# u's second half in split passes, its weights folded by adding transfers, and a table of places for every side step

## The chip, the cores and the metric

The kernel runs on one core of a Trainium2 chip. The metric is the device time in microseconds of one launch. A core has TensorE (PE: matmuls into PSUM; loads of the stationary operand are shown as PEld), VectorE (DVE), ScalarE (ACT), GpSimd (POOL) and the queue engine SyncE (SP). Each engine works off its own instructions in the order in which the program issues them; semaphores order the engines among each other.

## What is computed

One layer of a Fourier token mixer with a gate, for 512 latent tokens and, as a sequence of its own, 128 context tokens; the width is 1024.

```
h    = rms_norm(x, w) * (1 + scale) + shift        # scale, shift, gate = silu(cond) @ w_mod + b_mod
u, z = split(h @ w_in, 2, axis=-1)                 # 1024 columns each
y    = real(fft2(u, over positions and the 256 channels of each of 4 groups)) * silu(z)
x    = x + gate * (y @ w_out)
```

Inputs and outputs are fp32. The attention layer of the reference isn't run (DEPTH is 1).

## The kernel before, in words

**Precision.** PE takes a product of fp32 operands in several passes of its own. The kernel instead splits most operands into a high and a low part of type fp32r (ACT casts the high part, DVE subtracts to get the low one) and runs three passes: high by high, low by high, high by low. `high_piece` and `low_piece` do this for a piece of weights, `plain` and `plain_low` for h, `split_u`, `split_y` and `split_mid` for u, y and the middle channels. Only u's products run on plain fp32 operands (`product_u`, L606).

**Pieces.** The weights are cut into 48 pieces of 128 rows by 512 columns (256 KB): pieces 0 to 7 and 8 to 15 give z's two halves, 16 to 23 and 24 to 31 u's, 32 to 39 and 40 to 47 the output projection. The code's program order is one long list of products by piece `n`, and between them the places `(n, i)`: `run(n, i)` issues there whatever was put in by `at(n, i, step, ...)`. These lists of side steps are written by hand. In z's second half pieces 8 to 11 run one after the other; of 12 to 15 the second token halves of all four column tiles come first (places (12, j) and (13, j)), then the first token halves (places (14, j) and (15, 4j + n - 12)).

**Fold and Fourier transform.** For u the transform over positions is taken ahead of the product with the weights. The tokens (`xn`, five tiles) are scaled by their norms, folded into sums and differences of mirrored positions, four times for 256 columns each (`fold_first`, `fold_context`, `fold_pair`, `fold_cos`, `fold_even`, `fold_sin`), split into fp16 parts (`fold_split`), and `sequence(k)` multiplies 128 columns by the tables (`load_tables`); `evacuate(k)` scales the result into the tile `xs[k]`, 642 columns of bins and shifts. The norms come from `square` (ACT, one for each token tile) and `rms` (POOL). `spread_rms` (L478) writes the 640 norms to DRAM and reads them back as rows, on SP, and `order_rms` (POOL) puts them in order. `shift_products` and `turn_shifts` give the shift term of z; `take_halves` copies z's second half out of PSUM and so frees its banks, of which two serve the first `sequence`.

**u's weights.** u's channels are taken as sums and differences of mirrored channels, so each of its pieces must be folded: `fold_piece` (L202) takes a loaded piece and lets DVE write the sum of its two halves and their difference into one of four slots of the tile `folded`. Before that, `folded` holds rows of weights for `weigh_tile` (DVE, the shift by products and sums, steps 2, 3, 6 and 7). `fold_piece` then issues the load of the piece five further on.

**After u.** `take_u` copies u out of PSUM, `shift_u` adds the mean term, `channels(g)` transforms over the channels, for each of four groups: three passes each for cosine and sine and two for the middle channel (L701), with the high and the low part of `mid`. `channel_out`, `channel_last`, `mix` and `split_y` make the operand of the output projection. `scale_z` and `silu_z` finish z, `weigh_gate` (DVE, with `load_gate`) and `gates` the gate, `results` and `finish_halves` add x and write the result.

## Time and profile before

| | us |
|---|---|
| median of 3 runs | 187.64 (187.57 to 187.74) |
| the profiled execution | 187.82 |
| its span, first to last instruction | 186.0 |
| busy in it: PE, DVE, ACT, POOL | 180.7, 144.9, 87.9, 17.4 |

The profile lists instructions by line and engine with their busy time and mean duration in ns, and what ended the idle time before them. A timeline row reads: start, length, engine, line, operation, output tile <- input tiles, shapes, count, and in brackets the idle time before it with its releaser. In a timeline several like instructions are merged into one row, so that the spacing of rows shows what one really takes from the engine; durations are longer, since the end of one overlaps the start of the next. SPq rows are the issue of a transfer; a transfer's time from issue to landing stands in the list of DMA issues. Stages are marked by the times at which products of new pieces begin.

### The profile page before, as it was taken

What the parts mean: (1) busy time and instruction counts of PE and PEld (TensorE: products, weight loads), DVE (VectorE), ACT (ScalarE), POOL (GpSimd) and SP (SyncE); (2) the same over time, 40 slices, a digit from 0 to 9 for tenths busy, and PEclk for the clock granted to TensorE, in tenths of its full rate; (3) what the DMA queues carried; (4) which work ended last, traced back from release to release, by engine and by line L of the source; (5) the groups of instructions that cost most, each with busy time, mean ns of one, the idle gap of its engine ahead of it and who ended that gap; (6) DMA issues with size and microseconds to landing.
All of it is one profiled execution on the core that took longest, in us unless ns stands there. A gap on an engine that the chain in (4) does not pass through costs nothing.

```text
span 186.0 us, 3224 instructions
## 1 busy us (share of the span) xinstructions
PE 180.7 (97%) x1146; PEld 147.3 (79%) x1146; DVE 144.9 (78%) x319; ACT 87.9 (47%) x199; POOL 17.4 (9%) x56
## 2 busy tenths in 40 slices
PE   7999999999999998999999999999999999999993
PEld 2677777789999988877685786768868889999992
DVE  0544468998999999799998795589869969999422
ACT  3153743359960056977446446778774035210000
POOL 3000000010061005500012031020110000000000
PEclk9999999999999999999999999999999999999999
DMA  5999999999953007843258143120322453703532
GB/s 178 344 406 409 402 402 405 397 389 403 346 156 113 0 10 185 260 188 115 61 221 323 61 113 113 11 104 0 116 60 56 167 176 116 262 16 146 209 119 93
DMA packets 15504, 35.58 MB, mean 191 GB/s; under 512 B 2432, under 2 KB 3200, under 8 KB 15360
## 3 DMA queue, kind: packets, MB, share of 16 engines
q1 hardware_dynamic: 15344, 35.33, 53.8%
q8 instruction: 9, 0.15, 0.4%
q10 hardware_dynamic: 144, 0.04, 0.1%
q14 instruction: 7, 0.06, 0.1%
HBM read 32.75 MB, written 2.62 MB: 190 GB/s over the span
## 4 chain that ended last, share of the span: by engine, by line
PE 73%; DVE 15%; ACT 6%; DMA 3%; issue 2%; SPq 1%; DVEq 0%
PE acc L363 25%; PE acc L610 14%; PE h L400 8%; PE s L400 8%; DVE junk L307 6%; PE acc L373 6%; PE pl L569 3%; DMA zs<-in_w_in 3%; DVE wl L220 3%; PE pm L290 2%; ACT zs L447 1%; PE pc L569 1%; PE acc L618 1%; ACT wh L213 1%; DVE shz L315 1%
## 5 line engine op out<-in xcount | busy, mean ns | idle before, releaser
L610 PE MATMUL acc<-x,folded 128*128 128x324 f32 (+1 forms) x128 | 36.9, 438 | 0.0
L610 PEld LDWEIGHTS acc<-x,folded 128*128 128x128 f32 x128 | 23.5, 190 | 9.6 <-issue 1.0
L220 DVE TENSOR_TENSOR wl<-ws,wh 128x512 fp32r<-128x512 f32 x27 | 18.0, 687 | 2.8 <-ACT wh L213 2.8
L213 ACT CAST wh<-ws 128x512 fp32r<-128x512 f32 x27 | 16.3, 617 | 7.7 <-PE h L400 7.7
L307 DVE SCALAR_TENSOR_TENSOR junk<-wg,cb 128x1024 bf16<-128x1024 f32 x16 | 19.5, 1221 | 0.3
L301 DVE TENSOR_SCALAR a<-pm,b_scale,nw 128x2 f32<-128x2 f32 x8 | 2.2, 278 | 14.6 <-PE pm L300 14.5
L363 PE MATMUL acc<-yh,wh 128*128 128x512 f32 x32 | 13.0, 408 | 0.1
L363 PE MATMUL acc<-yl,wh 128*128 128x512 f32 x32 | 12.6, 394 | 0.0
L363 PE MATMUL acc<-yh,wl 128*128 128x512 f32 x32 | 12.6, 394 | 0.0
L334 ACT ACTIVATE hh<-xt,a 128x128 fp32r<-128x128 f32 (+1 forms) x15 | 7.5, 546 | 9.4 <-DVE a L301 9.4
L400 PE MATMUL h<-yh,wh 128*128 128x256 f32 (+1 forms) x40 | 11.0, 292 | 0.0
L400 PE MATMUL h<-yl,wh 128*128 128x256 f32 (+1 forms) x40 | 11.0, 292 | 0.0
L400 PE MATMUL h<-hl,wh 128*128 128x256 f32 (+1 forms) x40 | 11.0, 292 | 0.0
L400 PE MATMUL h<-hh,wl 128*128 128x256 f32 (+1 forms) x40 | 11.0, 292 | 0.0
L400 PE MATMUL h<-hh,wh 128*128 128x256 f32 (+1 forms) x40 | 11.0, 292 | 0.0
L400 PE MATMUL h<-yh,wl 128*128 128x256 f32 (+1 forms) x40 | 11.0, 291 | 0.0
L363 PE MATMUL acc<-hh,wl 128*128 128x512 f32 x32 | 11.0, 419 | 0.0
L307 DVE SCALAR_TENSOR_TENSOR junk<-folded,cb 128x1024 bf16<-128x1024 f32 x8 | 9.8, 1221 | 0.1
L307 DVE SCALAR_TENSOR_TENSOR junk<-wr,cb 128x1024 bf16<-128x1024 f32 x8 | 9.8, 1219 | 0.1
L363 PE MATMUL acc<-hh,wh 128*128 128x512 f32 x32 | 9.4, 417 | 0.4 <-DVE wh L213 0.4
L363 PE MATMUL acc<-hl,wh 128*128 128x512 f32 x32 | 9.2, 394 | 0.0
L341 DVE SCALAR_TENSOR_TENSOR hl<-xt,a,hh 128x512 fp32r<-128x512 f32 (+1 forms) x16 | 8.1, 549 | 1.4 <-ACT hh L334 1.4
(213 smaller groups left out, 457.8 us busy)
## 6 DMA issues: line engine op xcount, KB each, us to landing
ws<-in_w_in SPq DMA_DIRECT2D x27, 256.0 KB, 4.2
wg<-in_w_rows SPq DMA_DIRECT2D x8, 512.0 KB, 3.3
ws<-in_w_out SPq DMA_DIRECT2D x16, 256.0 KB, 2.8
wm<-in_w_scale SPq DMA_DIRECT2D x7, 512.0 KB, 8.1
xt<-in_x_t SPq DMA_DIRECT2D x8, 320.0 KB, 7.7
xn<-in_x_nat SPq DMA_DIRECT2D x5, 512.0 KB, 7.0
out<-o SPq DMA_DIRECT2D x7, 320.0 KB, 2.2
wr<-in_w_rows SPq DMA_DIRECT2D x4, 512.0 KB, 7.2
```

The source lines that it names most:

```text
L213: copy(hi, raw[n])
L220: engine.tensor_tensor(lo, t, hi, op=ALU.subtract)
L290: nc.tensor.matmul(pm[32 * j : 32 * j + 32, 0:P], cs[:, ko, :], wm[k][:, ko, :], start=ko < 4, stop=ko >= 4)
L301: nc.vector.tensor_scalar(a8[:, k, :], m, b_scale[:, k : k + 1], nw8[:, k : k + 1], ALU.add, ALU.mult)
L307: nc.vector.scalar_tensor_tensor(junk, w, 1.0, cb[:, D * j : D * j + D], ALU.mult, ALU.mult, accum_out=out)
L334: nc.scalar.activation(hs[k][0][:, cols], xt[:, k, cols], AF.Identity, scale=a8[:, k, j : j + 1])
L341: nc.vector.scalar_tensor_tensor(hl[:, cols], xt[:, k, cols], a8[:, k, j : j + 1], hh[:, cols], ALU.mult, ALU.subtract)
L363: nc.tensor.matmul(chunk(n // KT)[f], w_[:, P * f : P * f + P], x_[:, 0:SL], start=first and i == 0, stop=last and i == 1,)
L373: nc.tensor.matmul(chunk(n // KT)[4], x_[:, SL:T], w_, start=first and i == 0, stop=last and i == 1)
L400: nc.tensor.matmul(half(c, f, j), w_[:, P * f : P * f + P], x_[:, tokens(c)[j]], start=first and i == 0, stop=last and i == 2,)
L569: nc.tensor.matmul(out[:, cols], fold[name][x][:, kk], t[:, at + cols.start : at + cols.stop], start=n == 0 and not add, stop=n == 2 and n ...
L610: nc.tensor.matmul(chunk(n // KT)[f][:, 0 : cols.stop - cols.start], raw[n][:, P * f : P * f + P], xs[n % KT][:, cols], start=first, stop= ...
```

## The change

Three things are changed together.

1. **u's second half.** For pieces 24 to 31 `high_piece` and `low_piece` now split the folded weights, the new `split_x` splits `xs[k]` into a high and a low part, and `product_u` runs three passes of split operands in place of one fp32 product. Pieces 16 to 23 stay in fp32.
2. **Folding by transfers.** `fold_load` (SP) loads the second 256 columns of a piece into the first half of its slot in `folded`; `fold_negate` (ACT) writes their negative into the second half; `fold_piece` (issued from POOL) is a transfer that adds the first 256 columns from DRAM to both halves. DVE no longer folds, and SP no longer loads whole pieces for u.
3. **Places.** All side steps stand in one table, `PLAN`, of (n, i, step, arguments), in the order of issue at each place. Many steps are broken into finer ones (`silu_z` and `weigh_gate` by condition, the folds into their parts).

Besides, `split_mid` puts the high part and, in the rows that hold a copy of the middle weights, the low part into one operand, so that `channel` runs one pass for the middle channel in place of two.

```
 PLAN = (                                  # new; the places around the end of z and in u
     (8, 1, "high_piece", 9), (8, 1, "high_piece", 10), (8, 3, "weigh_tile", 3), (8, 3, "square", 2),
     (8, 3, "square", 4), (8, 3, "high_piece", 13), (8, 3, "low_piece", 9), (8, 3, "low_piece", 10),
     (8, 3, "high_piece", 11), (8, 3, "weigh_tile", 4), (9, 1, "low_piece", 11), (9, 1, "low_piece", 13),
     (9, 1, "weigh_tile", 5), (9, 1, "square", 3), (9, 1, "square", 1), (9, 2, "square", 0),
     (9, 3, "high_piece", 15), (9, 3, "open_x", 2), (9, 3, "high_piece", 14), (9, 3, "rms"),
     (10, 0, "open_folds"), (10, 0, "low_piece", 15), (10, 1, "high_piece", 12), (10, 1, "load_shift", 7),
     (10, 1, "low_piece", 14), (10, 1, "low_piece", 12), (10, 1, "weigh_tile", 6), (10, 3, "spread_rms"),
     (11, 2, "fold_first", 0), (11, 2, "fold_load", 17), (11, 2, "fold_load", 16), (11, 2, "fold_context", 0),
     (11, 2, "weigh_tile", 7), (11, 2, "fold_pair", 0, 1), (11, 2, "fold_pair", 0, 0), (11, 2, "fold_cos", 0),
     (11, 2, "order_rms"), (11, 3, "fold_load", 19), (12, 0, "fold_context", 2), (12, 1, "fold_negate", 17),
     (12, 1, "open_x", 3), (12, 1, "open_x", 4), (12, 1, "fold_sin", 0), (12, 1, "fold_even", 0),
     (12, 2, "fold_negate", 16), (13, 3, "fold_split", 0, "c"), (13, 3, "shift_products", 0),
     (14, 0, "fold_split", 0, "so"), (15, 0, "fold_split", 0, "co"), (15, 0, "shift_products", 1),
     (15, 0, "fold_first", 1), (15, 0, "fold_split", 0, "se"), (15, 1, "take_halves", 2, 1),
     (15, 1, "take_halves", 0, 1), (15, 3, "fold_split", 0, "ce"), (15, 4, "fold_pair", 1, 1),
     (15, 5, "load_tables"), (15, 5, "open_x", 0), (15, 5, "fold_pair", 1, 0), (15, 5, "take_halves", 3, 1),
     (15, 5, "fold_cos", 1), (15, 5, "fold_piece", 16), (15, 5, "fold_context", 1), (15, 9, "fold_load", 18),
     (15, 10, "take_halves", 3, 0), (15, 11, "take_halves", 0, 0), (14, 3, "open_x", 1),
     (14, 3, "fold_negate", 18), (14, 3, "sequence", 0), (14, 3, "fold_first", 2), (14, 3, "take_halves", 1, 0),
 ...
     (14, 3, "turn_shifts"),
     (14, 3, "evacuate", 0), (14, 3, "fold_split", 1, "c"), (15, 12, "load_piece", 36),
     (15, 12, "fold_negate", 19), (15, 14, "take_halves", 1, 1), (15, 15, "sequence", 1),
 ...
     (21, 4, "fold_negate", 24), (21, 4, "fold_piece", 24), (21, 4, "fold_load", 25), (21, 4, "fold_piece", 23),
 ...
     (23, 1, "fold_negate", 25), (23, 1, "high_piece", 24), (23, 1, "split_x", 5), (23, 1, "silu_z", 0, 1),
 ...
     (43, 4, "weigh_gate", 5, 1), (43, 4, "weigh_gate", 6, 0), (43, 4, "low_piece", 47),
     (43, 4, "weigh_gate", 6, 1), (43, 4, "weigh_gate", 7, 0), (43, 4, "weigh_gate", 7, 1), (43, 4, "gates"),
     (43, 4, "results", 2), (43, 4, "results", 3), (43, 4, "results", 1), (43, 4, "results", 0),
 )
```

```diff
+    def fold_load(n):
+        if 2 * KT <= n < 4 * KT:
+            c, k = place(n)
+            raw[n] = folded[:, 512 * (n % 4) : 512 * (n % 4) + 512]
+            nc.sync.dma_start(raw[n][:, 0:256], a["w_in"][c, k][:, 256:512])
+
+    def fold_negate(n):
+        if 2 * KT <= n < 4 * KT:
+            nc.scalar.mul(raw[n][:, 256:512], raw[n][:, 0:256], -1.0)
+
     def fold_piece(n):
-        t = raw[n]
-        raw[n] = folded[:, 512 * (n % 4) : 512 * (n % 4) + 512]
-        nc.vector.tensor_tensor(raw[n][:, 0:256], t[:, 0:256], t[:, 256:512], op=ALU.add)
-        nc.vector.tensor_tensor(raw[n][:, 256:512], t[:, 0:256], t[:, 256:512], op=ALU.subtract)
-        load_piece(n + 5)
+        if not 2 * KT <= n < 4 * KT:
+            return
+        c, k = place(n)
+        both = raw[n].rearrange("p (j f) -> p j f", j=2)
+        nc.gpsimd.dma_start(
+            both, a["w_in"][c, k][:, 0:256].unsqueeze(1).to_broadcast([P, 2, 256]), accum_op=ALU.add
+        )
...
+    def split_x(k):
+        tag = "al" if k < 4 else "ah"
+        xhigh[k], xlow[k] = (xpool.tile([P, X_COLS], F32R, name=f"x{q}{k}", tag=tag) for q in "hl")
+        x, hi, lo = (t[:, 0:X_END] for t in (xs[k], xhigh[k], xlow[k]))
+        nc.scalar.copy(hi, x)
+        nc.vector.tensor_tensor(lo, x, hi, op=ALU.subtract)
...
-        nc.tensor.matmul(
-            chunk(n // KT)[f][:, 0 : cols.stop - cols.start],
-            raw[n][:, P * f : P * f + P], xs[n % KT][:, cols], start=first, stop=last,
-        )
+        k = n % KT
+        pairs = three(n, (xhigh[k], xlow[k])) if n in wsplit else ((raw[n], xs[k]),)
+        for i, (w_, x_) in enumerate(pairs):
+            nc.tensor.matmul(
+                chunk(n // KT)[f][:, 0 : cols.stop - cols.start], w_[:, P * f : P * f + P], x_[:, cols],
+                start=first and i == 0, stop=last and i == len(pairs) - 1,
+            )
...
-        for i in range(2):
-            nc.tensor.matmul(out, ch[0][:, tb], mid[i][:, COS], start=False, stop=i == 1)
+        nc.tensor.matmul(out, ch[0][:, tb], mid[1][:, COS], start=False, stop=True)
```

For comparison, the places before around the end of z:

```
 (8, 0, square, 0, 1), (8, 3, square, 2), (8, 3, load_tables), (9, 2, square, 3), (9, 3, square, 4), (9, 3, rms),
 (10, 0, spread_rms), (10, 1, fold_first, 0), (11, 2, fold_pairs, 0),
 (12, 1, fold_split, (0, "co", "so", "c", "ce", "se")), (14, 1, shift_products, 0, 1), (14, 1, order_rms),
 (14, 1, take_halves, (0, 1), (0, 0), (3, 1)), (14, 1, fold_piece, 16), (14, 3, turn_shifts), (14, 3, sequence, 0)
```

More of the change, by code (lines that the diff above doesn't have):

```diff
@@ L92, in channel_tables @@
         for row in range(0, 128, 32):
-            out[row + g, C_ODD + 128 * g : C_ODD + 128 * g + 128] = np.where(k % 2 == 0, 0.0, -2.0)
+            for part in (g, G + g):
+                out[row + part, C_ODD + 128 * g : C_ODD + 128 * g + 128] = np.where(k % 2 == 0, 0.0, -2.0)
     return out.astype(np.float32)
@@ L254, in condition @@
         nc.gpsimd.tensor_scalar(nw8, small[:, 2 * KT : 3 * KT], 2.0**-X_BITS, None, ALU.mult)
-        nc.gpsimd.tensor_copy(w_mid_s[:, :, 0:G], w_mid)
+        for part in range(2):
+            nc.gpsimd.tensor_copy(w_mid_s[:, :, G * part : G * part + G], w_mid)
     accs = {}
@@ L780, in result, with results @@
         )
+    def results(d):
+        for j, cols in ((1, slice(0, SL)), (0, slice(SL, T))):
+            result(d, j, cols, zs[:, d, cols])
+        write(d)
     def write(d, cols=slice(0, T)):
@@ L1059, in fourier_step @@
         run(n, 4)
-    gates()
-    for d in range(4):
-        results(d)
     for f in range(4):
         for i in range(2):
+            run(44, 2 * f + i)
             for n in range(44, 48):
```

214 lines of the change are left out of this document (95 added, 119 removed).

## Prediction

> **What bounds the kernel now.** I read the page first, then the busy times by stage, then each engine's queue in order of time around the steps that move.
>
> ```profile
> span 186.0 us, 3224 instructions
> PE 180.7 (97%) x1146; PEld 147.3 (79%) x1146; DVE 144.9 (78%) x319; ACT 87.9 (47%) x199; POOL 17.4 (9%) x56
> ```
>
> TensorE is the bound, and an average hides little here, as the stages show (columns: PE, PEld, DVE, ACT, POOL busy, clock, DMA share, GB/s):
>
> ```profile
> 59.00:76.30 17.30, 16.71 (x141) 15.03 (x140) 16.82 (x47) 7.51 (x22) 4.61 (x16) 1.00 0.32 74
> 76.30:101.40 25.10, 25.10 (x177) 18.35 (x174) 23.21 (x58) 15.54 (x37) 1.87 (x7) 1.00 0.55 188
> 101.40:122.40 21.00, 21.00 (x92) 14.65 (x92) 15.04 (x35) 13.21 (x35) 2.46 (x7) 1.00 0.35 105
> ```
>
> The stages are the end of z's second half, then u's first half (pieces 16 to 23) and u's second half (24 to 31). In both of u, PE never idles: work taken off PE there shortens the kernel, if ACT and DVE keep up. Before them PE idles once, at the hand-over:
>
> ```profile
> 57.25 0.28 PE L400 MATMUL h<-hh,wh 128*128 128x256 f32 x1
> ...
> 71.16 0.33 PE L400 MATMUL h<-hh,wl 128*128 128x386 f32 x1
> 72.08 1.05 PE L426 MATMUL h<-small,shifts 128*128 128x2 f32 x8 [0.59 <-ACT zs L447]
> ...
> 77.10 1.31 PE L610 MATMUL acc<-x,folded 128*128 128x324 f32 x4
> ```
>
> z's last four pieces start at 57.25, three of four groups are over at 71.3, and piece 16 starts at 77.10. That hand-over is the dangerous place, because the queue that loads weights stands still just ahead of it:
>
> ```profile
> 42.81 0.42 SPq L193 DMA_DIRECT2D xn<-in_x_nat  x1
> ...
> 57.26 0.39 SPq L481 DMA_DIRECT2D rms_row<-r  x1
> 68.38 0.34 SPq L484 DMA_DIRECT2D rt<-rms_row  x1
> 68.77 1.32 SPq L484 DMA_DIRECT2D rb<-rms_row  x1
> 70.21 4.40 SPq L185 DMA_DIRECT2D ws<-in_w_in  x4
> ```
>
> spread_rms writes 640 numbers to DRAM and reads them back, and SP waits from 57.26 to 68.38 for the write to land. Loads issued behind it in the program come out at 70.21. Today nothing near needs them.
>
> **Part by part: what PE saves.** In u's second half a 324-column fp32 product becomes three passes of split operands.
>
> ```profile
> 107.20 0.31 PE L686 MATMUL pb<-uh,ch_l 128*128 128x318 f32 x1
> ...
> 108.08 0.31 PE L701 MATMUL pa<-midl,ch_h 128*128 128x322 f32 x1
> ...
> 115.02 7.83 PE L610 MATMUL acc<-x,folded 128*128 128x318 f32 x28
> 122.44 0.64 PE L363 MATMUL acc<-yh,wh 128*128 128x512 f32 x1
> ```
>
> From 107.20 to 108.08 are six split passes of this width, each with other weights: 0.147 us a pass, 0.44 for three. The 28 records are 14 products (fp32 leaves two each): 7.42/14 = 0.53 us. Saved 0.09 x 32 = 2.9 us. channel drops one 322-column pass in each of four groups, 0.147 each: 0.3 us in this stage, 0.3 in the next. PE gains 3.2 us here.
>
> **What the side engines pay in u's second half.**
>
> ```profile
> L206 DVE TENSOR_TENSOR folded<-ws 128x256 f32<-128x256 f32 x16 | 6.9, 428 | 1.4 <-PE acc L610 1.4
> L220 DVE TENSOR_TENSOR wl<-ws,wh 128x512 fp32r<-128x512 f32 x27 | 18.0, 687 | 2.8 <-ACT wh L213 2.8
> ```
>
> DVE loses two 256-column operations for a piece (2 x 0.43) and gets one 512-column one (0.69), and for each of eight x tiles a 642-column one (about 0.86, by columns). In this stage that is five folds out (-4.3), six pieces and two x tiles in (+5.9): 15.0 becomes 16.6, under PE's new 17.8 (21.0 less 3.2). ACT gets six casts (0.52 each, below), two 642-column casts (0.65) and five negations of 256 columns (0.30 as a cast, 0.40 as a scaled activation; I take 0.35): 13.2 + 3.1 + 1.3 + 1.8 = 19.4. So ACT passes PE by 1.6 us. Some of its work (silu, the casts for w_out) is placed past the stage, so the give-back may be 0; I take the full 1.6, because ACT also has to wait in order for transfers. In u's first half ACT has 15.5 of 25.1 us, gets eight negations (2.8), six x casts (3.9) and two piece casts (1.0), 23.2 in all: covered by PE's 25, with no cover left to spare.
>
> **The new weight path.** Each u piece is now a 128 KB load on SP into a slot of `folded`, a negation on ACT, and an adding transfer issued from Pool. No such transfer is in the trace.
>
> ```profile
> xn<-in_x_nat SPq DMA_DIRECT2D x5, 512.0 KB, 7.0
> ws<-in_w_out SPq DMA_DIRECT2D x16, 256.0 KB, 2.8
> out<-o SPq DMA_DIRECT2D x1, 128.0 KB, 1.7
> rms_row<-r SPq DMA_DIRECT2D x1, 2.5 KB, 11.1
> ```
>
> It writes 256 KB: at least 1.7, at most twice the plain 256 KB load, 5.6; I take 3.5, near the 2.8 of the row of its size. In u's first half a slot is free three pieces ahead (about 9 us) and load, negation and addition take some 6: hidden. In the second half piece 25's slot comes free only after piece 21, and each us over 3.5 delays ACT's cast by as much: 0 to +2. The Trainium skill, "DMA: Bandwidth & Descriptors", section "Anatomy of one DMA — SWDGE (gpsimd) path", fits 2.0 us plus bytes over 436e3 to a transfer issued by Pool, 2.6 us for this one as an estimate; by it the give-back would be up to 0.9 less. No run here shows it.
>
> **What ACT waits for before u: the decisive step.** In the new table the loads of pieces 17 and 16 stand at place (11, 2), behind spread_rms at (10, 3) on SP, and their negations at (12, 1) and (12, 2), ahead of every split of the first fold, both shift copies and all take_halves on ACT. When do those loads come?
>
> ```profile
> 49.49 1.14 ACT L213 CAST wh<-ws 128x512 fp32r<-128x512 f32 x2
> 50.52 1.06 ACT L472 ACTIVATE squares<-xn 128x1024 bf16<-128x1024 f32 x1
> ...
> 51.58 0.61 ACT L213 CAST wh<-ws 128x512 fp32r<-128x512 f32 x1
> ```
> ```profile
> 51.76 0.25 POOL L475 TENSOR_SCALAR ss<-ss 128x5 f32<-128x5 f32 x1 [13.34 <-ACT squares L472]
> ...
> 53.52 1.43 POOL L600 COPY x<-shz 128x2 f32<-128x2 f32 x3
> ```
>
> The square of the last token tile, today ACT's fifth, becomes its second. That tile is issued at 42.81 and lands 7.0 later, 49.8; ACT stands until then. After it come that square (1.06), two casts (0.52 each), three squares (3.2): 55.1. Pool takes 1.8 for the roots: 56.9, and SP writes the row about when it does today. From the row's issue to the next load was 12.95 us (57.26 to 70.21): loads of 17 and 16 at 69.8 and 70.2. They land 1.7 to 4.2 us later; 3.0 is my value, nearer the upper end because the read-back is still running: 72.8. Only then does ACT go on, with these jobs, each by the spacing of its row:
>
> ```profile
> 68.31 0.40 ACT L548 CAST se_h<-se 128x256 f16<-128x256 f32 x1
> 68.61 0.91 ACT L519 ACTIVATE y<-xn,r 128x256 f32<-128x256 f32 x2
> 69.43 0.49 ACT L523 ACTIVATE xn<-xn,r 128x256 f32<-128x256 f32 x1
> 69.83 0.62 ACT L421 COPY shifts<-h 128x256 f32<-128x256 f32 x2
> 70.34 0.37 ACT L447 COPY zs<-h 128x256 f32<-128x256 f32 x1
> 70.61 0.49 ACT L447 COPY zs<-s 128x386 f32<-128x386 f32 x1
> 70.98 0.39 ACT L447 COPY zs<-h 128x256 f32<-128x256 f32 x1
> ```
>
> Two negations 0.7, five splits at 0.30, two y 0.82, one context 0.40, two shift copies 0.51, three 256-column halves at 0.27, two 386-column ones at 0.37: 5.5 us, to 78.3. sequence(0) needs the splits and the two PSUM banks that the last two copies free, so PE waits for all of it. PE comes there at 71.3 + 0.6 (weigh_tile 3 now stands ahead of low_piece 9, and low_piece 12 behind 15 and 14: DVE hands these two over 0.2 and 0.4 late). It waits 6.4 us. What follows up to piece 16 is the 5.0 us from 72.08 to 77.10: piece 16 at 83.3, +6.2. The seq tables, now issued behind these loads too, land before 78.3 by the same latencies. Of Pool's queue, order_rms still waits for the read-back, and the first addition follows at about 77: landed by 81, hidden behind the same wait.
>
> So long a pause also has a price in clock:
>
> ```profile
> 184.00:185.00 1.00, 0.00 (x0) 0.00 (x0) 0.00 (x0) 0.00 (x0) 0.00 (x0) 1.00 0.39 131
> 185.00:186.00 1.00, 0.00 (x0) 0.00 (x0) 0.00 (x0) 0.00 (x0) 0.00 (x0) 0.67 0.00 0
> ```
> ```profile
> 1.19 3.17 PE L274 MATMUL spare<-idle 128*128 128x512 f16 x7 [1.19 <-DVE idle L237]
> ```
>
> PE runs nothing in either of these two rows, which lie behind its last product, and in the second the granted clock falls: a pause of a few us is enough. At the start seven 512-column passes took 3.17 us, 0.45 each; 3.17 us at half clock lose 1.6 us. Between 0 and 2; I take 1.6.
>
> **The sum**, against this execution (187.82 = span 186.0 + 1.8 around it; the median of the three is 0.18 lower): hand-over +6.2, clock +1.6, second half -3.2 + 1.6, the next stage -0.3 for channel and -0.3 for a take_u that PE no longer meets late. At the end weigh_gates crowd on DVE, five of them ahead of the results:
>
> ```profile
> L307 DVE SCALAR_TENSOR_TENSOR junk<-wg,cb 128x1024 bf16<-128x1024 f32 x16 | 19.5, 1221 | 0.3
> ```
>
> That is 6.1 us, and over it lie the last four pieces' products, 48 passes of two halves at about 0.147: 14.1 us. Nothing, then; without that cover it would be the 6.1. Together +5.6: 193.4 by this execution, 193.2 by the median.
>
> **Rivals.** *The row lands early* (0.17). One execution shows 11.1 us for 2.5 KB; the other rows here put even 128 KB at 1.7. If it lands in about 2, load 17 comes out when weigh_tile 6 has freed its slot (about 61), lands by 64, ACT is done in time, PE does not wait, and piece 16 starts near 76.5. Sum -0.6 - 1.6 - 0.6 on 187.6: 184.8, faster. It decides at a landing of piece 17 near 66.4 (PE's 71.9 less 5.5); each us later costs one. Against it: SP's idle time of 10.7 us is in the trace, and no edit touches those transfers. The Trainium skill's fit ("DMA: Bandwidth & Descriptors", the same section) would put 2.5 KB at 2.0 us; the trace's 11.1 disagrees, and the measurement decides.
>
> *No wait there, but ACT and the additions eat the gain* (0.06): additions at 5.6 us give back 2.1 beside ACT's 1.6, 3.7 in all against 0.6 + 3.2 + 0.6: 186.9; if the first half's pieces are held up once as well, by the same 2.1, it is 189.0.
>
> *A short wait* (0.05): ACT reaches its squares sooner, the row goes out near 53, as Pool's rows today would allow; load 17 lands at 69, ACT is through at 74.5, PE waits 2.6 with no loss of clock, piece 16 starts at 79.5, +2.4 against -2.2: 187.8.
>
> **How the numbers follow.** Main case 0.72, from 188.7 (landing in 1.7, no clock loss, all of the stage's gain kept: 4.5 less) to 196.9 (4.2, clock 2, additions at 5.6: 3.7 more). With the cases near no change the range reaches from 186.0 to 196.5; the early landing and the very top are left out. Under 0.2% (0.4 us) the measurement can't tell. Faster 0.17 + 0.02, same 0.05, slower 0.72 + 0.04.
>
> **What would show it.** ACT's negation of piece 17 idle before it for over 10 us, released by the load; PE idle about 6 us before sequence(0), with PEclk under 1 behind it; piece 16 near 83 to 85; u's second half 18 to 19 us with ACT busiest. Piece 16 at 77 or less makes the forecast wrong, as does a row landing in 2 to 5 us.

## The result, and the profile after

The changed kernel takes 209.09 us (median of 5 runs, 208.51 to 209.69) beside 187.64 us before (5 runs, 187.57 to 188.11): 1.1135 times as long, 95% interval 1.111 to 1.116. Slower was forecast, by 5.6 us; it is slower by 21.4. The profiled execution has a span of 206.7 us where it was 186.0, so 20.7 us are to be found.

The page of the changed kernel: its head, the granted clock in 40 slices, and two groups that were not there before.

```profile
span 206.7 us, 3356 instructions
PE 187.0 (90%) x1174; PEld 154.8 (75%) x1174; DVE 145.3 (70%) x303; ACT 101.9 (49%) x231; POOL 35.8 (17%) x73
...
PEclk9999999999999975799998599996999999999999
...
L312 POOL DMA_DIRECT2D folded<-in_w_in x16 | 19.7, 1363 | 31.6 <-ACT folded L304 20.8
...
L304 ACT ACTIVATE folded<-folded 128x256 f32<-128x256 f32 x16 | 6.4, 415 | 16.8 <-DMA folded<-in_w_in 16.8
```

TensorE was busy for 180.7 of 186.0 us, and is for 187.0 of 206.7: 14.4 us more of standing, and 6.3 more of work although it has less to do. The second is the clock: three dips in the row of PEclk, where before there was none. No side engine is near full, so none of them is too slow as a whole; the two groups show what stands: ScalarE 16.8 us ahead of negations, for loads, and Pool 20.8 us ahead of adding transfers, for negations.

The stages by windows of the changed kernel, cut where z's last four pieces, piece 16, piece 24 and piece 32 start:

```profile
72.10:85.90 13.80, 8.53 (x51) 8.11 (x51) 8.60 (x23) 9.92 (x29) 6.08 (x15) 0.63 0.41 92
85.90:119.10 33.20, 28.09 (x171) 18.44 (x171) 21.07 (x43) 21.97 (x50) 10.96 (x13) 0.90 0.79 163
119.10:144.00 24.90, 20.22 (x117) 17.92 (x116) 14.49 (x27) 16.76 (x43) 7.70 (x13) 0.93 0.62 122
144.00:206.70 62.70, 59.58 (x335) 53.00 (x334) 52.95 (x104) 22.59 (x48) 4.66 (x10) 1.00 0.39 131
```

Piece 16 starts at 85.9 instead of 77.1 (+8.8), u's first half takes 33.2 instead of 25.0 (+8.2), its second 24.9 instead of 20.4 (+4.5), and the rest 62.7 instead of 63.6 (-0.8). These are the 20.7. For the kernel before, piece 24 is taken to start at 102.08 and piece 32 at 122.44 (the forecast's window for u's second half begins 0.7 us sooner, at 101.4, with the products of the middle weights):

```profile
102.08 5.13 PE L610 MATMUL acc<-x,folded 128*128 128x324 f32 x18
```

**The hand-over** went the way that the forecast describes. SyncE's queue, ScalarE's and TensorE's by order of time (the bracket is the idle time ahead, and what ended it):

```profile
56.88 0.39 SPq L589 DMA_DIRECT2D rms_row<-r  x1
65.52 0.34 SPq L592 DMA_DIRECT2D rt<-rms_row  x1
65.91 3.11 SPq L592 DMA_DIRECT2D rb<-rms_row  x1
69.12 1.33 SPq L300 DMA_DIRECT2D folded<-in_w_in  x3
70.50 0.43 SPq L281 DMA_DIRECT2D seq_h<-in_seq_h  x1
```
```profile
49.54 1.06 ACT L580 ACTIVATE squares<-xn 128x1024 bf16<-128x1024 f32 x1 [3.50 <-DMA xn<-in_x_nat]
...
72.19 0.72 ACT L304 ACTIVATE folded<-folded 128x256 f32<-128x256 f32 x2 [13.60 <-DMA folded<-in_w_in]
...
76.86 0.87 ACT L554 COPY zs<-s 128x386 f32<-128x386 f32 x2
```
```profile
77.41 0.27 PE L667 MATMUL pc<-seq_h,c_h 128*128 128x130 f16 x1 [5.27 <-ACT zs L554]
...
113.85 3.56 PE L718 MATMUL acc<-x,folded 128*128 128x324 f32 x6 [3.97 <-DMA folded<-in_w_in]
...
129.99 0.73 PE L817 MATMUL pb<-u,ch 128*32 128x322 f32 x4 [1.96 <-issue]
138.13 0.42 PE L718 MATMUL acc<-xh,wh 128*128 128x324 f32 x1 [2.33 <-ACT wh L319]
```

The row is issued at 56.88 (56.9 forecast), load 17 at 69.12 (69.8), ScalarE goes on at 72.19 (72.8) and TensorE at 77.41 after 5.27 us (78.3, 6.4). But of the four waits in the third fence only the first is in the hand-over. The second, 3.97 us ahead of piece 23, is for an adding transfer itself; for the third, 1.96 us, the profile shows no releaser; the last is for a cast whose input an adding transfer had just written. What the clock does behind them, in windows around each:

```profile
74.00:84.80 10.80, 7.39 (x40) 7.02 (x41) 7.99 (x22) 7.72 (x23) 3.15 (x6) 0.53 0.25 56
112.00:119.00 7.00, 5.15 (x15) 2.47 (x16) 3.40 (x8) 4.25 (x8) 2.15 (x3) 0.51 0.60 114
128.00:132.00 4.00, 2.04 (x14) 1.52 (x14) 2.52 (x5) 1.94 (x6) 0.00 (x0) 1.00 0.80 173
138.00:143.00 5.00, 4.67 (x18) 4.00 (x19) 3.33 (x5) 3.48 (x10) 0.00 (x0) 0.66 0.36 81
```

The share that the gate withheld of the time in which TensorE ran: 7.39 x 0.47 + 5.15 x 0.49 + 4.67 x 0.34 = 3.5 + 2.5 + 1.6 = 7.6 us, nothing at 130. With the idle time, 5.3 in the hand-over, 33.2 - 28.1 = 5.1 and 24.9 - 20.2 = 4.7 in the halves, it comes to 22.7. That is 2.0 more than the loss: the kernel before stood for 0.6 us in its hand-over, and TensorE's own work, at the full clock, is 1.3 us less than before (187.0 - 7.6 = 179.4 beside 180.7).

And the transfers: bytes, and the median from issue to landing.

```profile
folded<-in_w_in POOLq DMA_DIRECT2D x16, 256.0 KB, 5.4
...
folded<-in_w_in SPq DMA_DIRECT2D x16, 128.0 KB, 3.4
...
rms_row<-r SPq DMA_DIRECT2D x1, 2.5 KB, 8.5
```

An adding transfer takes 5.4 us where 3.5 was taken (5.6 had been the upper bound), and its half-size load 3.4.

### The profile page after: what moved, and what is told of

The parts are those of the page before. It is cut to its first block, busy times and chain, and to the rows that moved or that the text cites. A ratio compares the mean times of both kernels' runs of the same rounds, so it can differ in the third digit from the quotient of the medians.

```text
span 206.7 us, 3356 instructions
## 1 busy us (share of the span) xinstructions
PE 187.0 (90%) x1174; PEld 154.8 (75%) x1174; DVE 145.3 (70%) x303; ACT 101.9 (49%) x231; POOL 35.8 (17%) x73
## 3 DMA queue, kind: packets, MB, share of 16 engines
q0 software_dynamic: 4352, 4.20, 14.1%
## 4 chain that ended last, share of the span: by engine, by line
PE 61%; DMA 19%; issue 6%; ACT 5%; DVE 3%; POOL 2%; SPq 2%; POOLq 0%; ACTq 0%
PE acc L470 21%; PE acc L718 10%; DMA folded<-in_w_in 10%; PE s L507 8%; PE h L507 8%; PE acc L480 5%; DMA rms_row<-r 4%; DMA xn<-in_x_nat 3%; PE pl L667 3%; PE pm L397 2%; SPq L592 2%; DMA small<-in_small 2%; DVE wl L326 1%; DVE junk L414 1%; PE spare L381 1%
## 5 line engine op out<-in xcount | busy, mean ns | idle before, releaser
L718 PE MATMUL acc<-x,folded 128*128 128x324 f32 (+1 forms) x64 | 21.6, 476 | 4.3 <-DMA folded<-in_w_in 4.0
L312 POOL DMA_DIRECT2D folded<-in_w_in x16 | 19.7, 1363 | 31.6 <-ACT folded L304 20.8
L718 PEld LDWEIGHTS acc<-x,folded 128*128 128x128 f32 x64 | 12.3, 206 | 10.7 <-issue 7.6
L414 DVE SCALAR_TENSOR_TENSOR junk<-wg,cb 128x1024 bf16<-128x1024 f32 x16 | 19.5, 1221 | 0.5 <-DMA wg<-in_w_rows 0.4
L304 ACT ACTIVATE folded<-folded 128x256 f32<-128x256 f32 x16 | 6.4, 415 | 16.8 <-DMA folded<-in_w_in 16.8
L718 PE MATMUL acc<-xh,wh 128*128 128x324 f32 (+1 forms) x32 | 11.1, 346 | 2.4 <-ACT wh L319 2.3
L718 PE MATMUL acc<-xh,wl 128*128 128x324 f32 (+1 forms) x32 | 10.9, 341 | 0.4 <-DVE wl L326 0.3
L705 DVE TENSOR_TENSOR xl<-x,xh 128x642 fp32r<-128x642 f32 x8 | 6.6, 825 | 5.7 <-ACT xh L704 5.7
```

Source lines behind the costliest of these rows:

```text
L304: nc.scalar.mul(raw[n][:, 256:512], raw[n][:, 0:256], -1.0)
L312: nc.gpsimd.dma_start(both, a["w_in"][c, k][:, 0:256].unsqueeze(1).to_broadcast([P, 2, 256]), accum_op=ALU.add)
L414: nc.vector.scalar_tensor_tensor(junk, w, 1.0, cb[:, D * j : D * j + D], ALU.mult, ALU.mult, accum_out=out)
L705: nc.vector.tensor_tensor(lo, x, hi, op=ALU.subtract)
L718: nc.tensor.matmul(chunk(n // KT)[f][:, 0 : cols.stop - cols.start], w_[:, P * f : P * f + P], x_[:, cols], start=first and i == 0, stop=l ...
```

## The experiments

Theory A is what the forecast and the trace together say: (1) SyncE's, ScalarE's and Pool's queues run in order, and the table puts waits for late transfers ahead of work that TensorE needs; (2) the adding transfers are too long to hide; (3) pauses cost a second time, in clock. Rivals: the table's other places or loaded side engines cost the time (B, D); Pool's issue or other traffic makes the transfers slow, not the adding (C, E); the chain of load, negation and addition is too long for four slots, in whatever order (F). Each time beside a run of the kernel before of 187.7 to 188.0 us on the same chip; one run each unless more are named. Entries of the table are given by their step alone.

**The transfers: adding or not.**

```
             both, a["w_in"][c, k][:, 0:256].unsqueeze(1).to_broadcast([P, 2, 256])
-            ..., accum_op=ALU.add
```

> Changed kernel with the transfers from Pool writing their 256 KB plainly, without adding to what is there (so the fold is left out: both halves of the slot hold the first half of the weights). Everything that waits still waits. Theory A (the adding itself makes the transfer slow): issue to landing falls from a median of 5.4 us to 2.5-3.5, the waits for additions go, u's first half takes 26-28 us instead of 33.2 and the second 21-22.5 instead of 24.9, the hand-over stays: 198 to 202. Rival C (a transfer issued by Pool, or any transfer in the traffic of this stage, takes that long): landing stays at 5 or more and the time at 206 to 209.

198.29 us, 10.8 less. Theory A's number, and C is out. The queue line of the page (packets, MB, share of 16 engines' span) and the issues, first of the changed kernel, then of this one:

```profile
q0 software_dynamic: 4352, 4.20, 14.1%
```
```profile
q0 software_dynamic: 1280, 4.20, 6.2%
...
folded<-in_w_in POOLq DMA_DIRECT2D x16, 256.0 KB, 3.5
```

The same bytes go in 1280 packets instead of 4352 and occupy the engines for 6.2% of 196.5 instead of 14.1% of 206.7 us: 0.76 instead of 1.8 us for each of sixteen. Landing falls from 5.4 to 3.5, the very value of the forecast. Whether it is the adding as such or the smaller packets that take the time, no run separates. U's second half takes 19.4 us (114.1 to 133.4), just over the 18 to 19 of the forecast and 1 us less than before; the first still takes 28.7, more than was expected of this run, and the hand-over is as late as ever. The Trainium skill, "DMA: Bandwidth & Descriptors", section "Anatomy of one DMA — SWDGE (gpsimd) path", gives 2.6 us for this size, as an estimate from its fit for transfers issued by Pool; neither run agrees, and the fit has no term that tells plain from adding.

**The hand-over.** First, ScalarE's negations behind the copies that free the banks:

```
-(12, 1) fold_negate 17, (12, 2) fold_negate 16                  from here
+(15, 11) take_halves 0 0, fold_negate 17, fold_negate 16        to here
```

> Changed kernel with the negations of pieces 17 and 16 moved on ScalarE behind the last copy that frees a PSUM bank for the sequence transforms. Theory A (in-order ScalarE waits behind the late loads; then PE pauses and its clock halves): PE's 5.3 us wait and the clock loss behind it vanish, piece 16 starts at 77.5 to 79.5 instead of 85.9, and the time falls by 4 to 8 us to 201-205 (not by all 8.8, because the next additions cannot be issued much sooner than now). Rival B (the new order of the other side steps sets the hand-over): piece 16 stays at 84 or later and the time at 207 to 209.

206.72 us. In this edit piece 16's addition stands ahead of its negation in program order, so that the slot ends up with another content than the fold. Piece 16 starts at 82.2, not at 77.5 to 79.5, and u's first half is longer than in the changed kernel (34.8 against 33.2 us): as a whole inconclusive. With the addition moved along:

```
+(15, 11) take_halves 0 0, fold_negate 16, fold_piece 16, fold_negate 17
```

> Changed kernel with piece 16's negation, its adding transfer and then piece 17's negation behind the last copy on ScalarE that the sequence transforms need. Theory A, as the first four runs leave it: ScalarE is out of the way at about 67, but the transforms' tables, issued behind the same read-back, land at 73.3, so TensorE still waits 1 to 2 us, and a short stretch of half clock follows; piece 16 at 79.5 to 82 (85.9 now), the time 203 to 206. If the negations were the whole of it: no wait, piece 16 at 77 to 78, 200 to 201.

204.36 us, piece 16 at 82.4. ScalarE is out of the way, and a wait appears that its delay had covered:

```profile
73.65 0.22 PE L667 MATMUL pc<-seq_h,c_h 128*128 128x130 f16 x1 [1.44 <-DMA seq_h<-in_seq_h]
74.34 0.22 PE L667 MATMUL pc<-seq_l,c_h 128*128 128x130 f16 x1 [0.42 <-DMA seq_l<-in_seq_l]
```
```profile
73.00:75.50 2.50, 1.43 (x19) 1.33 (x19) 0.00 (x0) 0.81 (x3) 2.15 (x7) 1.00 0.59 190
75.50:82.30 6.80, 6.80 (x34) 6.40 (x34) 4.12 (x12) 3.84 (x11) 4.34 (x6) 0.51 0.53 77
```

The transforms' tables stand behind the read-back too, and two short waits for them are followed by 6.8 us at half clock, 3.4 us lost. So the tables as well ahead of the row:

```
-(15, 5) load_tables
+(10, 3) load_tables, spread_rms
```

> As neg_late2, and the two tables of the sequence transforms are loaded ahead of the row of rms values instead of behind it. Theory A (everything issued behind the read-back is late, and two things of it are needed by the first transform): no wait ahead of the transform, no half clock behind it, piece 16 at 77 to 79, the time 200 to 202.5. If the tables do not matter: as neg_late2.

201.99 us, piece 16 at 79.0, no half clock before u: the hand-over gives back 6.9 of its 8.8. Theory A holds here. A third way leaves the table alone and moves the row to another queue:

```
 def spread_rms():
-    nc.sync.dma_start(...)        three times
+    nc.gpsimd.dma_start(...)
```

> Changed kernel, table and all, but the three transfers of the rms row go through Pool's queue, so that SyncE does not stand behind the row. Theory A (SyncE's place in order behind the row is the one cause of the hand-over's loss): weights of 17 and 16 and the tables are issued by 64, ScalarE's negations wait less than 3 us, the wait of 5.3 us and the half clock go, piece 16 at 77 to 79, the time 199 to 202.5, with u's two halves still near 33 and 25. If the order on ScalarE itself delays the copies: piece 16 at 81 or later.

206.61 us, a miss: the loads were issued early (60.45), and still did not land. ScalarE goes on at 70.0 instead of 72.2, TensorE stands for 3.06 us instead of 5.27, and piece 16 starts at 83.7, half clock ahead of it as before. Windows of this kernel, the last column GB/s:

```profile
60.00:64.00 4.00, 4.00 (x40) 3.78 (x43) 3.76 (x11) 0.00 (x0) 0.00 (x0) 1.00 0.03 9
64.00:68.00 4.00, 4.00 (x46) 3.15 (x39) 3.40 (x9) 0.00 (x0) 0.38 (x1) 1.00 0.07 15
68.00:72.00 4.00, 4.00 (x24) 3.86 (x22) 0.77 (x3) 1.99 (x7) 0.75 (x2) 1.00 0.85 291
```
```profile
57.23 1.14 POOL L589 DMA_DIRECT2D rms_row<-r  x1 [0.32 <-POOL r L584]
67.62 0.60 POOL L592 DMA_DIRECT2D rt<-rms_row  x1 [9.26 <-DMA rms_row<-r]
```
```profile
folded<-in_w_in SPq DMA_DIRECT2D x1, 128.0 KB, 9.5
```

While the row's 640 single numbers are on their way to DRAM (57.23 to 67.6), the loads issued from 60.45 on (four of 128 KB, the two tables, one of 256 KB) hardly move, all traffic together being 9 to 15 GB/s; then 291 follow. The first took 9.5 us for 128 KB. So SyncE's order is not the whole cause. What is issued beside this write lands no sooner than when it is through; what is issued ahead of it, as the tables in neg_tables, is there in time. That the write itself holds up the transfer engines is what the times suggest; no run here separates it.

**The three passes, with the old products in u's second half.** (No high and low parts of 24 to 31 and of x.)

```
-(...) high_piece 24 .. 31, low_piece 24 .. 31, split_x 0 .. 7
```

> Changed kernel with u's second half multiplied in fp32 as before (no high and low parts of pieces 24 to 31 and of the eight x tiles); adding transfers and table stay. Theory A (the second half is held up by late additions, with or without the casts behind them): PE pays 2.9 us more for the products and keeps most of its waits; the second half takes 23.5-26 us (24.9 now), the time 207 to 210. Rival D (casts and subtractions in ScalarE's and VectorE's queues hold it up): the second half is as before, 20.4 to 21.5 us, and the time 204 to 206.

219.22 us, and no evidence: without the casts the loads of 28 to 31 stand, in program order, ahead of the last products that read the pieces in these slots before, so those products use other weights and wait for a whole chain (TensorE stands 15.6 us for adding transfers). dve_fp32 below asks the question again.

**The folds by an engine instead of transfers.** On VectorE, in the slot, from one plain 256 KB load:

```
-    both, ... accum_op=ALU.add
+    u, v = raw[n][:, 0:256], raw[n][:, 256:512]
+    nc.vector.tensor_tensor(v, u, v, op=ALU.subtract)
+    nc.vector.scalar_tensor_tensor(u, u, 2.0, v, ALU.mult, ALU.subtract)
```

> Changed kernel with the folds computed by VectorE in the slot (difference over the second half, then twice the first half less the difference) from one plain 256 KB load, at the table's places; piece 16's fold stands behind the first sequence transform. No negations, no adding transfers. Theory A (the new weight path costs the time): no wait in the hand-over, piece 16 at 77 to 79; then VectorE is the bound, with 21.1 + 6.9 = 28 us in the first half and 14.5 + 6.9 = 21.4 in the second: 78 + 28 + 21.4 + 62.7 + 1.8 = 192, between 190 and 195. Rival B (the table's order costs it): 200 or more.

199.91 us, a miss, and only just under what rival B said. The sum missed the wait for the tables (2.90 us, first seen here) and 3.06 us for piece 24's low part, each with half clock behind it. The next run takes both away:

```
+(10, 3) load_tables, spread_rms
+(23, 2) low_piece 24, fold_piece 25          (24, 0) low_piece 25, fold_piece 26
```

> As dve_fold (folds computed by VectorE, no adding transfers), and the tables are loaded ahead of the rms row, and the low part of piece 24 is taken ahead of the fold of 25 (that of 25 ahead of the fold of 26) on VectorE. Theory A: the 2.9 us wait for the tables and 3.1 us for piece 24's low part go, with 3.4 and 1.7 us of halved clock behind them: 199.9 - 11 = 189, between 186.5 and 191. If VectorE is the bound with the folds on it: 193 to 196.

193.32 us, piece 16 at 77.2, the clock at 1.00 throughout. The wait is gone, but VectorE is the bound, as the rival said; windows of the two halves, the third busy time VectorE's. The second window ends 3 us ahead of the half: piece 32 starts at 128.98, and VectorE is busy up to there, so that the second half takes 23.8 us.

```profile
77.20:105.20 28.00, 25.48 (x172) 17.48 (x170) 26.07 (x60) 18.82 (x41) 0.87 (x3) 1.00 0.43 140
105.20:126.00 20.80, 16.61 (x97) 13.63 (x95) 19.22 (x43) 14.30 (x35) 4.80 (x10) 1.00 0.28 90
```

From that, u's second half in fp32 again, with the loads of 28 to 31 behind the products that free their slots:

```
-high_piece 24 .. 31, low_piece 24 .. 31, split_x 0 .. 7
+(25, 0) fold_load 28    (26, 0) fold_load 29    (27, 0) fold_load 30    (28, 0) fold_load 31
```

> As dve_early (193.3 us: folds on VectorE), but u's second half in fp32 as before: no high and low parts of pieces 24 to 31 and of the x tiles; the loads of 28 to 31 stand behind the products that free their slots. Theory A (with the folds back on it, VectorE is the bound of u's two halves, and three passes give VectorE and ScalarE more work than they save TensorE): TensorE pays 2.9 us more, VectorE 12 us less: 187 to 190.5. If TensorE or ScalarE bounds dve_early: 195 or more.

190.78 us, just over the range: 2.5 less than with three passes. With the folds on VectorE the passes take more than they give. The 2.8 us that remain over the kernel before on the same chip come without the three passes and without adding transfers. On Pool instead, from plain loads into w_out's tiles (the tables ahead of the row, and piece 23's fold, as it happens, ahead of 22's):

```
+    nc.gpsimd.tensor_tensor(raw[n][:, 0:256], t[:, 0:256], t[:, 256:512], op=ALU.add)
+    nc.gpsimd.tensor_tensor(raw[n][:, 256:512], t[:, 0:256], t[:, 256:512], op=ALU.subtract)
```

> Changed kernel with the tables ahead of the rms row and the folds as a sum and a difference of 256 columns each on Pool, from plain 256 KB loads into the tiles that w_out's first pieces are loaded into early (those loads stand behind piece 31's here); no negation, no adding transfer. Theory A (transfers that add are the cost of the halves; three passes are right if nothing else is late): if Pool takes about 1 us for each of 32 operations, they hide; u's first half 25.3 to 27 us, the second 18 to 20.5, the time 185 to 189. If Pool takes 2 us or more each, Pool is the bound: 64 us for u's 16 pieces, over 200.

198.36 us, a miss of 9 us, though Pool took what was assumed (0.90 and 0.92 us an operation). VectorE's operations became longer; two neighbours of one form on it:

```profile
80.49 0.41 DVE L657 TENSOR_TENSOR ce_l<-ce,ce_h 128x256 f16<-128x256 f32 x1
80.83 0.94 DVE L657 TENSOR_TENSOR so_l<-so,so_h 128x256 f16<-128x256 f32 x1
```

0.41 us alone, 0.94 beside a fold on Pool: the two take turns. The low parts of the weights of u's second half, 0.69 us each in the changed kernel, take 0.67 to 3.33 here, 1.12 on average, VectorE is busy for 28.3 of the 33.1 us of the first half, and TensorE's waits for it end in a stretch of half clock there (98.9 to 105.6). The Trainium skill, "SBUF — State Buffer", section "SBUF: two separate sides", states just this, a shared pair of ports locked for a whole instruction, for VectorE with two operands in SBUF beside a Pool operation that reads SBUF; the trace agrees. The sum on Pool and the difference on VectorE:

```
-    nc.gpsimd.tensor_tensor(..., op=ALU.subtract)
+    nc.vector.tensor_tensor(..., op=ALU.subtract)
```

> As pool_fold, with the sum on Pool and the difference on VectorE. Theory A: VectorE has about 22.7 of 25.3 us in the first half and 17 of 18 in the second, Pool half of what it has in pool_fold; 186 to 190; slower than pool_fold if VectorE's place in order delays the pieces, faster if Pool's operations are long.

192.02 us, a miss of 2, but better than either engine alone, and still over the kernel before.

**Why u's halves are long with adding transfers.** In the changed kernel piece 23's negation is done at 103.4, but its addition stands behind 24's negation (104.92) and addition on Pool, is issued at 106.35 and lands at 113.61. So, on neg_tables:

```
-(21, 4) fold_piece 23
+(20, 0) fold_negate 23, fold_piece 23
```

> As neg_tables (202.0 us), and piece 23's adding transfer stands right behind its negation, ahead of piece 24's load, negation and addition instead of behind them. Theory A (an addition of 4 to 8 us is late when it stands in order behind another piece's): the wait of 4.5 us ahead of piece 23 and the 3 us of half clock behind it go: 194 to 197. Rival E (the additions are slow because other transfers crowd them, whatever their order): at least 2 us of wait stay there, 198 or more.

202.02 us, the same to 0.03 as neg_tables. The addition now stood ahead of piece 22's, and the pause, 5.65 us, came before 22. So each of 18 to 25 and 28 right behind its own negation:

```
+(14, 3) fold_negate 18, fold_piece 18    ...    (25, 1) fold_negate 28, fold_piece 28
```

> As neg_tables (202.0 us), and the adding transfers of pieces 18 to 25 and 28 each stand right behind their own negation, in the order in which the pieces are multiplied. order_23 put 23's ahead of 22's as well and only moved the wait. Theory A (order): TensorE's waits for pieces 22 and 23 sink under 1.5 us, no half clock in u's first half, which takes 26 to 28.5 us instead of 33.7: 195 to 198. Theory F (the chain of one slot is too long whatever the order: load 3.4, negation 0.4, issue 1.2, addition 5.4 and the product 2.4 are 12.8 us for four pieces of 3.1): 25.6 us or more, with waits of 1 to 2 us spread over the pieces, and the same 195 to 198 if no pause is long, over 199 if one still is.

200.83 us, a miss. The first half falls from 33.7 to 29.0 us, no half clock in it, as order would have it; but the second grows from 24.9 to 28.6. And the order is not yet that of the pieces: 17's addition, left at (16, 1), now stands behind those of 18 and 19 on Pool (the row of three), and TensorE stands for 2.84 us ahead of piece 17:

```profile
75.79 3.76 POOL L312 DMA_DIRECT2D folded<-in_w_in  x3
```
```profile
84.77 2.94 PE L718 MATMUL acc<-x,folded 128*128 128x324 f32 x10 [2.84 <-issue]
```

One part of the change alone on the kernel before, load, negation and addition in place of VectorE's folds:

```
+    nc.sync.dma_start(raw[n][:, 0:256], a["w_in"][c, k][:, 256:512])     one piece after the slot is free
+    nc.scalar.mul(raw[n][:, 256:512], raw[n][:, 0:256], -1.0)
+    nc.gpsimd.dma_start(both, ..., accum_op=ALU.add)
```

> The kernel before with one part of the change alone: the folds by a load of the second half, a negation and an adding transfer (load one piece after its slot is free; the additions about where the folds stood). Fp32 products, the old order of all else. Theory F: the slots' chain of 12.8 to 13 us bounds four pieces, so u's first half takes 26 to 29 us (25.0 before), the second 25 to 28 (20.4 before), and the loads of 16 and 17, issued behind the rms row, cost the hand-over 1 to 5: 196 to 203. If the chain hides: under 191.

192.98 us, 5 us slower: less than F's number, and over the 191 of a hidden chain. The halves take 26.8 and 24.1 us (25.0 and 20.4 before), with waits of 0.3 to 1.7 us, no half clock, and no loss in the hand-over (piece 16 at 77.1), where no negation stands ahead of a copy and the tables are loaded early. So the adding folds alone, in the old order and with the old products, cost 5 us of the 21; the rest comes with the new order and the three passes, which this run leaves out. For prompt's second half, ScalarE's queue shows how, and gives theory G (the order on ScalarE):

```profile
121.02 0.62 ACT L319 CAST wh<-folded 128x512 fp32r<-128x512 f32 x1 [2.22 <-DMA folded<-in_w_in]
...
123.87 0.62 ACT L319 CAST wh<-folded 128x512 fp32r<-128x512 f32 x1 [1.16 <-DMA folded<-in_w_in]
...
124.72 0.72 ACT L304 ACTIVATE folded<-folded 128x256 f32<-128x256 f32 x2
```

The negations of 30 and 31, which start the next two additions, stand behind two casts that wait for the last two. So, ahead of those casts:

```
+(26, 4) low_piece 27, fold_load 31, fold_negate 30, fold_piece 30, high_piece 28
+(27, 1) fold_negate 31, fold_piece 31, high_piece 29
```

> prompt (200.8 us) with, on ScalarE, the negations of pieces 30 and 31 (and their additions on Pool) ahead of the casts of 28 and 29, and 31's load right behind piece 27's subtraction. Theory G (in u's second half the casts wait for additions, and the negations that start the next additions stand behind them in order on ScalarE, so that the additions go one after the other): 30's addition is issued 3 to 5 us sooner, the 2.4 us wait ahead of piece 30 and the half clock behind it go: 197 to 198.5. Theory F (the chain of a slot, or the transfers themselves, are the limit): 200 to 201.5.

197.99 us, as Theory G expected. In this kernel the same negations, at 121.31 and 124.17:

```profile
121.31 0.42 ACT L304 ACTIVATE folded<-folded 128x256 f32<-128x256 f32 x1 [1.02 <-DMA folded<-in_w_in]
121.74 0.62 ACT L319 CAST wh<-folded 128x512 fp32r<-128x512 f32 x1
...
124.17 0.42 ACT L304 ACTIVATE folded<-folded 128x256 f32<-128x256 f32 x1 [0.74 <-DMA folded<-in_w_in]
```

Piece 30's addition is issued at 122.0 instead of 125.4, and the second half is back at 25.1 us, without the pause before piece 30. A wait of 1.93 us for piece 24's low part stays, with 6.8 us of half clock behind it (111.3 to 118.1).

**Do the causes add up?** neg_tables with plain transfers (no accum_op):

> neg_tables (202.0 us) with the transfers from Pool writing plainly as in plain_add (so the fold is left out: both halves of the slot hold the first half of the weights). Theory A (two causes that add up: the hand-over's queue order, worth 7.1 us, and the time of the adding, worth 10.8): 209.1 - 7.1 - 10.8 = 191.2, between 189.5 and 192.5, with no wait for a transfer over 2 us. If the two overlap (waits of the halves that the later start had hidden): 194 or more.

190.59 us (191.2 forecast): the queue order of the hand-over and the adding add up as separate causes, the longest wait for a transfer is 1.9 us, and with both gone 2.7 us over the kernel before are left. Piece 16 starts at 78.8 (+1.7), the halves take 27.5 (+2.5) and 19.5 (-0.9), the rest 63.1 (-0.5).

**What TensorE's saving is worth.** On the kernel before, only the mid channel's pass (with what it needs in the tables and in split_mid, as in the change), 12 runs beside 17 of before:

```
-        for i in range(2):
-            nc.tensor.matmul(out, ch[0][:, tb], mid[i][:, COS], start=False, stop=i == 1)
+        nc.tensor.matmul(out, ch[0][:, tb], mid[1][:, COS], start=False, stop=True)
```

> The kernel before with another part of the change alone: one pass of split operands in place of two for the mid channel in each of the four groups. Theory A: TensorE is the bound where it runs and has no waits there, so each of the four passes is worth its 0.147 us: 0.6 us less, 187.0 to 187.3 beside 187.6 to 187.8; below half of it if VectorE or ScalarE bounds the place.

187.18 us beside 187.73, ratio 0.997, 95% interval 0.9958 to 0.9982. That agrees with 0.147 us in each of four groups, and this kernel beats both. And with u's last two pieces in three passes:

```
+(28, 2) split_x 6, (28, 3) high_piece 30, (29, 0) low_piece 30
+(29, 3) split_x 7, high_piece 31, (30, 0) low_piece 31
```

> As before_mid, and u's last two pieces (30 and 31) in three passes of split operands, with plain loads and folds on VectorE as before. Theory A: 8 products at 0.09 us saved are 0.7 us less, since VectorE (15.0 of 21 us there, and 3.1 more) and ScalarE (13.2, and 2.3 more) have the room: 186.2 to 186.8. Rival D (casts and subtractions come late in the queues of ScalarE and VectorE): 187.5 or more.

190.20 us, ratio to before 1.014, interval 1.0115 to 1.0164 (6 runs): 3.0 us slower than without, as rival D said. In the profiled executions 1.4 us of it lie in u's halves (46.4 us from piece 16 to piece 32, 45.1 without), where three passes wait for casts and subtractions, and 1.6 behind them: VectorE hands over u's last copies late, and TensorE waits for their bank. That wait, and the windows from 122.5 us of before_mid and then of this kernel:

```profile
126.60 0.50 PE L366 MATMUL acc<-yh,wh 128*128 128x512 f32 x1 [1.74 <-DVE u L668]
```
```profile
122.50:145.00 22.50, 22.39 (x102) 17.57 (x101) 20.10 (x40) 15.06 (x34) 2.93 (x10) 1.00 0.17 48
```
```profile
122.50:145.00 22.50, 20.76 (x97) 16.26 (x96) 19.92 (x41) 16.26 (x37) 3.04 (x10) 1.00 0.22 59
```

In the stage just behind, VectorE has 20 of 22.5 us to do; what is added in front of it seems to be pushed into it.

## Why the forecast had the sign and not the size

- **The hand-over** (+6.2 and clock +1.6 forecast, +8.8 measured). Right, to the order of the queue, the releaser and the place: neg_late2 and neg_tables take it away step by step. The clock was mis-sized, 1.6 against 3.5 us, the wait a little over (6.4 against 5.3). The 1.6 was half of a stretch of 3.17 us from the kernel's start, for which the profile shows a clock of 1.00; behind the pause the half clock lasted to 84.8, over 7.4 us of work. The tables "land before 78.3" was right and hid that they are late themselves. The row took 8.5 us to land, not 11.1, and rms_pool shows that SyncE's order is not all that keeps the loads back while it is on its way; the rival of an early row did not happen. The Trainium skill's fit ("DMA: Bandwidth & Descriptors", the section named above) that the forecast set beside the row is one for transfers issued by Pool; with Pool issuing the row (rms_pool) it took 10.1 us, so that the fit disagrees there too.
- **The new weight path, first half: the step that failed.** "In u's first half a slot is free three pieces ahead (about 9 us) and load, negation and addition take some 6: hidden." They take 3.4 + 0.4 + 5.4 = 9.2, and each hop waits in an in-order queue besides. Measured +8.2 instead of 0. Of this 4.5 us go with the adding (28.7 instead of 33.2 in plain_add), and 4.7 of the 33.7 in neg_tables with the order of the additions (29.0 in prompt): the two overlap. Even at the 3.5 us that were taken, 3.7 were not hidden (2.5 in plain_tables). The price was in the range that I gave for the adding transfer (1.7 to 5.6), but the middle of it was taken for the sum, and its upper end was charged to the first half only in a rival of 0.06, for one hold-up of 2.1 us. With 5.6 and the 3.0 taken for a load, the step comes to 9.0: no cover left.
- **Second half** (-3.2 + 1.6 forecast, +4.5 measured). With transfers of the assumed 3.5 us, plain_add has 19.4 us in this stage where 18 to 19 were forecast. A pass that need not wait costs 0.147 us as taken, but TensorE's busy time in the half falls only from 20.3 to 18.6 us there, 1.7 instead of 3.2: passes behind a short wait for a cast or subtraction follow each other in 0.2 to 0.5 us. ScalarE did not pass TensorE by its busy time (16.8 of 24.9 us); in the queue of prompt its negations stood in order behind casts that waited for additions, and neg_first takes 3.5 us of the half away by turning that round: an order that the forecast looked for in the hand-over and nowhere else.
- **The clock** was charged once. It came three times, 7.6 us in all.
- **The rest** (-0.6 forecast, -0.8 measured) and the end (nothing) held; before_mid agrees with channel's part.
- What stays open: the 2.7 us of plain_tables and the 2.8 of dve_fp32, with short waits for ScalarE and VectorE in the new order, were not taken apart; nor what exactly holds the transfers up beside the row's write.

## What to carry to other kernels

A chain that passes through three in-order queues and two transfers must be summed at the upper bounds of its terms, and against the time of a free slot, before it is called hidden; where it isn't, look at each queue for a wait that stands ahead of the step that starts the next chain. When a table of side steps is rewritten, write down for each queue what is issued behind a slow transfer and what beside it. Moving the bound engine's work to other engines did not pay here, where these had no room in that stage or the one behind it; one pass in each group dropped outright (0.6 us) beat all that was moved.

## What the runs showed of the hardware

- A pause of TensorE is paid twice, but not by its length alone. Waits of 5.3, 4.0 and 2.3 us were followed by half clock in the changed kernel, one of 1.96 us was not, but one of 1.93 us was in neg_first (6.8 us at half); 1.44 and 0.42 us among the short products of the hand-over were (neg_late2, 6.8 us at half), and 2.84 us ahead of piece 17 were not in prompt:

```profile
82.00:85.00 3.00, 0.23 (x1) 0.26 (x2) 0.83 (x3) 1.19 (x3) 0.00 (x0) 1.00 0.67 177
85.00:92.00 7.00, 6.55 (x50) 4.85 (x50) 4.99 (x12) 4.09 (x12) 2.38 (x4) 1.00 0.72 176
```

  The Trainium skill, "TensorE: Matmul & The Clock Gate", section "What's actually happening", puts a free-running window of about 3.4 us behind it, half rate after an idle window and full rate after a busy one. Stretches of 6.8 us (neg_late2, and 112 to 118.9) and 3.4 us (139.4 to 142.8) agree with multiples of it, and so does a 2.84 us pause that goes unpunished; 1.44 or 1.93 us that are punished do not fit a window that must be idle throughout.
- An adding transfer of 256 KB takes 5.4 us to land, the plain one from the same queue 3.5; the adding one goes in 3.4 times as many packets.
- 2.5 KB written to DRAM as single numbers take 8.0 us (before_add) to 11.1 us (before) to land, and 10.1 us from Pool's queue (rms_pool); while they were on their way there, all traffic was 9 to 15 GB/s, though loads stood issued (291 followed).
- A 256-column subtraction of VectorE takes 0.41 us, and 0.94 beside a fold of Pool (pool_fold).
